# Half-size weight tiles, splits ordered by a clock in the source, and an x scaled by its norm's factor, in a two-layer decoder trunk on one core

## The chip, the cores and the metric

The kernel runs on one core of one Trainium2 chip. A core has a matrix engine (TensorE, PE in the profile, with its weight loads as PEld), a vector engine (DVE), an activation engine (ACT), GpSimd (POOL) and a queue that issues transfers (SP, shown as SPq). Each engine works through its own list of instructions in the order in which the source emits them, and waits on semaphores where one needs the result of another. The metric is the time of one execution on the device in microseconds (us); lower is better.

## The reference

Two layers are applied to 256 tokens of 1024 columns, all in float32. What matters here:

```python
for i in range(DEPTH):
    g = norm_gains[i]
    f = swiglu(rmsnorm(h, g[0]), ffn_gate[i, 0], ffn_up[i, 0], ffn_down[i, 0])
    h = h + MACARON * rmsnorm(f, g[1])
    mix = hybrid_mixer(rmsnorm(h, g[2]), ...)
    h = h + rmsnorm(mix, g[3])
    f = swiglu(rmsnorm(h, g[4]), ffn_gate[i, 1], ffn_up[i, 1], ffn_down[i, 1])
    h = h + MACARON * rmsnorm(f, g[5])
    gate = jax.nn.sigmoid(rmsnorm(h, g[6]) @ w_ple_gate[i])
    h = h + rmsnorm((p[i].astype(h.dtype) @ w_ple[i]) * gate, g[7])

def swiglu(x, w_gate, w_up, w_down):
    return (jax.nn.silu(x @ w_gate) * (x @ w_up)) @ w_down
```

A gated unit (`swiglu`) has weights of 1024 x 2816 (gate, up) and 2816 x 1024 (down); there are four of them. `rmsnorm` divides a row by its root mean square, so the factor is one number for each token.

## The kernel before

**Precision.** Every float32 product is made from three matmuls (`mm3`, L320). A weight tile `raw` (128 partitions x 1024 values) is split into a piece `hi` (ACT, L152) and a piece `lo` = raw - hi (DVE, L153); the activations are split likewise into `xh` and `xl` while they are transposed (`split_t`, L392: four transposes on PE, `hi` by ACT at L401, `lo` by DVE at L402). The product is xh*hi + xh*lo + xl*hi.

**Weights.** The class `Weights` (L97) streams them in the order of their use. There are four raw tiles of 1 MB; one load fills a tile with two pieces, and a tile is loaded anew when both have been split. A split piece lives in a slot: eight pairs of tiles, and two further pairs made from tiles that the mixer uses (L235), which are shut while the mixer runs. `need` splits a piece at once if a matmul is about to use it; `tick` splits the next one if a slot is free. Which step of which phase has a tick, and at which step other work is inserted, is written out by hand in the table `PLAN` (L52), and `run` (L325) follows it.

**A gated unit** (`ffn`, L433) goes over six chunks of the 2816 hidden columns: five of 512 and one of 256. T = 2 token tiles t of 128 rows. In each chunk of 512 there are six phases of 24 matmuls: gate t = 0 and 1 (pieces G0 to G3, two blocks of 128 inputs each), up t = 0 and 1 (U0 to U3), down t = 0 and 1 (D0 to D3). A phase runs in 8 steps of three matmuls; a slot comes free when the phase of t = 1 has used its piece. Gate ends in `silu` on ACT (L448), up in `hm` on DVE (L453); both multiply by `rx[t]`, the norm's factor of each token, because x itself is not scaled by it. `hid_t` transposes hm for the down phase.

The four units start in two ways. Unit 1 of layer 0 ("start") runs gate 0, gate 1, up 0, up 1 in its first chunk and has two insertions from the beginning of the program (`enter(1)` with the transposes of the second token tile). The other three ("first") run gate 0, up 0, gate 1, up 1, with the three insertions of `pending` (L388) that are left from the sublayer before. In them, gate 0 puts its xl matmuls last (`lo_last`, L418), with steps of two matmuls. After the first chunk of unit 1, `setup_late` (L289) loads masks and makes the rotary tables on DVE and ACT.

**Mixer and gate of the embeddings** (`mixer` L537, `ple` L774) use `run` and `PLAN` for their order, and the same slots.

```python
def tick(self):
    if self.can():
        self.prepare()
...
h1 = lambda: hid_t(1, hm1, nb)
if first:
    gate(0, c, pend[0], lo_last=True)
    hm0 = up(0, c, pend[1], pend[2])
    gate(1, c, h0)
    hm1 = up(1, c)
```

Of the kernel before, what the change touches and what calls it, by code (L numbers as in the profile page):

```python
# [36 lines left out]
NRAW = 4  # L37
CHUNKS = [(0, 512), (512, 512), (1024, 256), (1280, 512), (1792, 512), (2304, 512)]
# [58 lines left out]
class Weights:  # L97
# [3 lines left out]
    def __init__(self, nc, raw_pool, slots):  # L101
# [3 lines left out]
        self.shut = set()  # L105
        self.slot = {}
        self.specs = []
        self.loads = []
        self.raw = {}
        self.got = {}  # L110
        self.next = 0
        self.next_load = 0

    def add(self, keys, src, a, n):
        load = len(self.loads)
        self.loads.append((src, a * len(keys), n))
        for i, key in enumerate(keys):
            self.specs.append((key, load, i, a, n, i == len(keys) - 1))

    def load_one(self):  # L120
        i = self.next_load
        if i >= len(self.loads):
            return
        src, a, n = self.loads[i]
        raw = self.raw_pool.tile([P, 2048], F32, tag="raw", name=f"raw{i}")
        view = raw[:, : a * n].rearrange("p (a n) -> p a n", n=n)
        if i == 0:
            for j in range(0, a, a // 2):
                self.nc.sync.dma_start(view[:, j : j + a // 2], src[:, j : j + a // 2])
        else:  # L130
            self.nc.sync.dma_start(view, src)
        self.raw[i] = view
        self.next_load += 1

    def pick(self):
        return next((i for i in self.free if i not in self.shut), None)

    def can(self):
        return self.next < len(self.specs) and self.pick() is not None

    def prepare(self):
        key, load, part, a, n, last = self.specs[self.next]
        while self.next_load <= load:
            self.load_one()
        raw = self.raw[load][:, part * a : (part + 1) * a, :]
        slot = self.pick()
        self.free.remove(slot)
# [3 lines left out]
        hv, lv = (v.rearrange("p (a n) -> p a n", n=n) for v in (hi, lo))  # L151
        self.nc.scalar.activation(hv, raw, AF.Copy)  # L152
        self.nc.vector.tensor_tensor(lv, raw, hv.bitcast(F32), op=ALU.subtract)  # L153
        self.got[key] = (hv, lv)
        self.next += 1
        if last:
            del self.raw[load]
            self.load_one()
# [4 lines left out]

    def need(self, key):
        while key not in self.got:
            assert self.can(), (key, self.specs[self.next])
# [9 lines left out]
def hybrid_block(ctx: ExitStack, tc: tile.TileContext, a, out):  # L176
# [53 lines left out]
    ones = const.tile([1, P], F32, name="ones")  # L230
    nc.gpsimd.memset(ones, 1.0)

# [1 line left out]
    slots = [((piece_pool, f"hi{i}", 1024), (piece_pool, f"lo{i}", 1024)) for i in range(NS)]  # L234
    slots += [((work, "kdt", 1024), (work, "grp", 1024)), ((work, "vm", T * H * VW), (work, "vd", T * H * VW))]  # L235
    W = Weights(nc, raw_pool, slots)
    for l in range(DEPTH):
        for f in range(2):
            if f == 1:
# [3 lines left out]
                def add_in(name, c0, n):  # L243
                    for j in range(2):
                        W.add([(l, name, 2 * j), (l, name, 2 * j + 1)], win[:, 4 * j : 4 * j + 4, c0 : c0 + n], 2, n)

                add_in("A", 0, ZA)
                add_in("dq", ZA, 512)
                W.add([(l, "qu", 0), (l, "qu", 1)], a["w_q_up"][l].rearrange("(k p) n -> p k n", p=P), 1, 768)
                W.add([(l, "kvu", 0)], a["w_kv_up"][l].rearrange("(k p) n -> p k n", p=P), 1, 1024)  # L250
                add_in("dk", ZA + 512, 512)
                add_in("dv", ZA + 1024, 512)
                for half in range(2):
                    for n in range(2):
                        W.add([(l, "wo", half, n, 0), (l, "wo", half, n, 1)],
                              wo[:, 4 * half : 4 * half + 4, n * 512 : (n + 1) * 512], 2, 512)
            wg = a["ffn_gate"][l, f].rearrange("(k p) n -> p k n", p=P)
            wu = a["ffn_up"][l, f].rearrange("(k p) n -> p k n", p=P)
            wd = a["ffn_down"][l, f].rearrange("(k p) n -> p k n", p=P)
            for c, (f0, w) in enumerate(CHUNKS):  # L260
                ka = 1024 // w
                for name, src in (("G", wg), ("U", wu)):
                    for j in range(KD // (2 * ka)):
                        W.add([(l, f, c, name, 2 * j), (l, f, c, name, 2 * j + 1)],
                              src[:, 2 * ka * j : 2 * ka * (j + 1), f0 : f0 + w], ka, w)
                for j in range(w // 256):
                    k0 = f0 // P + 2 * j
                    W.add([(l, f, c, "D", 2 * j), (l, f, c, "D", 2 * j + 1)], wd[:, k0 : k0 + 2, :], 1, 1024)
        gt = a["w_ple_gate"][l].rearrange("(k p) n -> p k n", p=P)
        for n in range(2):  # L270
            for j in range(2):
                W.add([(l, "gt", n, 2 * j), (l, "gt", n, 2 * j + 1)],
                      gt[:, 4 * j : 4 * j + 4, n * 512 : (n + 1) * 512], 2, 512)
            if n == 0:
                W.add([(l, "pe", 0), (l, "pe", 1)], a["w_ple"][l].rearrange("(k p) n -> p k n", p=P), 1, 1024)

    for i in range(NRAW):
        if i == 2:
# [10 lines left out]
    def setup_late():  # L289
        """Masks and rotary tables."""  # L290
# [51 lines left out]
    def rstd(ss, ns, tag="rs", eps=EPS):  # L342
        """(ss / n + eps) ** -0.5 for each column of ss."""
# [25 lines left out]
    def post(t, f, gain, q, gain_pre):  # L369
        """h[t] += norm(f) / q; gives h[t] * gain_pre, and what does the second half of the columns."""  # L370
# [36 lines left out]
    def proj(ps, t, keys, fin, cols=None, k0=0, first=True, last=True, sh=None, sl=None, lo_last=False):  # L407
        """ps += x[t] @ w over the pieces named by keys."""
# [4 lines left out]
        for i, key in enumerate(keys):  # L413
            wh, wl = W.need(key)
            na = wh.shape[1]
            for j in range(na):
# [493 lines left out]
```

## Time and profile before

| | |
|---|---|
| median of the runs | 1053.22 us (2 runs, 1052.02 and 1054.42) |
| span of the profiled execution | 1052.4 us |
| PE busy | 1037.1 us, 5168 matmuls |
| PEld busy | 867.0 us |
| DVE busy | 645.8 us, 819 instructions |
| ACT busy | 528.9 us, 744 instructions |
| POOL busy | 51.1 us |
| transfers | 189.02 MB, mean 180 GB/s |

The times are of one profiled execution, in microseconds from its first instruction. The page gives no time of this execution other than its span; the span lies between the two timed runs, 0.8 us below their median. A row of a group gives line, engine, operation, output and inputs by the program's names, how many, the busy time and the mean of one in ns, and the idle time of that engine just before, with what ended it. A row of a timeline gives the start, the length, and the instruction; rows of the same instruction in succession are merged ("x4"), and idle time before it stands in brackets.

### The profile page before, as it was taken

Reading aid. Unit: us, or ns where it says so; the run is one execution under the profiler, and the core shown is the slowest. Engines: PE = TensorE matmul, PEld = TensorE weight load, DVE = VectorE, ACT = ScalarE, POOL = GpSimd, SP = SyncE. Lnnn points to the kernel's source line nnn. Section 1 sums busy time; section 2 is a strip of 40 time slices with the busy share of each in tenths; the row PEclk is TensorE's granted clock in tenths of the full one; section 3 lists DMA queues with packets and bytes.
Section 4 is the critical chain, followed back from the end, with each engine's and each line's share of the span. In section 5 each row is a group of like instructions: output and inputs, shape, how many; then the busy total and the mean of one; then the engine's idle time right before and its main releaser. Section 6 shows DMA issues by size and latency. Waiting matters only on the chain.

```text
span 1052.4 us, 13069 instructions
## 1 busy us (share of the span) xinstructions
PE 1037.1 (99%) x5168; PEld 867.0 (82%) x5168; DVE 645.8 (61%) x819; ACT 528.9 (50%) x744; POOL 51.1 (5%) x123
## 2 busy tenths in 40 slices
PE   8999999999999999999999999999999999999997
PEld 5889888878888898888878888888888888988886
DVE  4765554778677455456776545557877864555474
ACT  5544443555556444444665444445564654444463
POOL 0000000210020000000110000002000200000011
PEclk9999999999999999999999999999999999999999
DMA  8864546364227564554547645455532575545601
GB/s 321 304 227 168 193 164 211 106 222 160 82 94 272 191 213 160 201 200 160 200 160 259 212 169 200 153 163 168 180 120 82 190 275 184 198 162 172 227 21 40
DMA packets 86158, 189.02 MB, mean 180 GB/s; under 512 B 3665, under 2 KB 15313, under 8 KB 86098
## 3 DMA queue, kind: packets, MB, share of 16 engines
q1 hardware_dynamic: 86098, 188.20, 52.0%
q8 instruction: 40, 0.66, 0.2%
q14 instruction: 20, 0.16, 0.0%
HBM read 187.13 MB, written 1.05 MB: 179 GB/s over the span
## 4 chain that ended last, share of the span: by engine, by line
PE 92%; DVE 3%; ACT 2%; DMA 1%; issue 1%; POOL 0%; SPq 0%; DVEq 0%; POOLq 0%; ACTq 0%
PE acc L479 23%; PE u L323 8%; PE u L321 8%; PE u L322 8%; PE g L321 7%; PE g L323 7%; PE g L322 7%; PE tp L398 3%; PE o L706 2%; PE sc L666 1%; DVE lo L153 1%; PE gt L323 1%; PE gt L322 1%; PE gt L321 1%; PE f L321 1%; PE f L323 1%
## 5 line engine op out<-in xcount | busy, mean ns | idle before, releaser
L153 DVE TENSOR_TENSOR lo<-raw,hi 128x1024 fp32r<-128x1024 f32 (+1 forms) x338 | 405.1, 1214 | 204.2 <-ACT hi L152 194.1
L152 ACT ACTIVATE hi<-raw 128x1024 fp32r<-128x1024 f32 (+1 forms) x338 | 347.2, 1049 | 170.9 <-PE u L323 79.3
L479 PE MATMUL acc<-hi,hid 128*128 128x512 f32 x704 | 201.5, 392 | 0.0
L479 PEld LDWEIGHTS acc<-hi,hid 128*128 128x128 f32 x704 | 131.7, 188 | 27.4
L321 PE MATMUL u<-hi,xh 128*128 128x512 f32 (+1 forms) x384 | 145.3, 379 | 0.0
L323 PE MATMUL u<-hi,xl 128*128 128x512 f32 (+1 forms) x384 | 143.2, 373 | 0.0
L322 PE MATMUL u<-lo,xh 128*128 128x512 f32 (+1 forms) x384 | 143.0, 372 | 0.0
L321 PE MATMUL g<-hi,xh 128*128 128x512 f32 (+1 forms) x360 | 135.0, 375 | 2.3 <-ACT xh L401 2.3
L323 PE MATMUL g<-hi,xl 128*128 128x512 f32 (+1 forms) x360 | 134.6, 374 | 0.0
L322 PE MATMUL g<-lo,xh 128*128 128x512 f32 (+1 forms) x360 | 134.5, 374 | 0.0
L479 PE MATMUL acc<-lo,hid 128*128 128x512 f32 x352 | 118.3, 395 | 0.0
L323 PEld LDWEIGHTS u<-hi,xl 128*128 128x128 f32 x384 | 72.3, 188 | 13.0
L322 PEld LDWEIGHTS u<-lo,xh 128*128 128x128 f32 x384 | 72.4, 188 | 12.1
L321 PEld LDWEIGHTS u<-hi,xh 128*128 128x128 f32 x384 | 72.3, 188 | 12.0
L321 PEld LDWEIGHTS g<-hi,xh 128*128 128x128 f32 x360 | 68.5, 190 | 14.4 <-ACT xh L401 2.7
L322 PEld LDWEIGHTS g<-lo,xh 128*128 128x128 f32 x360 | 68.5, 190 | 12.3 <-DVE lo L153 0.5
L323 PEld LDWEIGHTS g<-hi,xl 128*128 128x128 f32 x360 | 68.4, 190 | 12.4 <-DVE xl L402 0.6
L479 PEld LDWEIGHTS acc<-lo,hid 128*128 128x128 f32 x352 | 66.2, 188 | 13.2
L401 ACT ACTIVATE hid<-tp 128x512 fp32r<-128x512 f32 (+1 forms) x48 | 27.0, 563 | 95.6 <-PE tp L398 95.6
L453 DVE SCALAR_TENSOR_TENSOR hm<-u,rs,silu 128x512 f32<-128x512 f32 (+1 forms) x48 | 33.7, 703 | 65.1 <-PE u L323 65.1
L448 ACT ACTIVATE silu<-g,rs 128x512 f32<-128x512 f32 (+1 forms) x48 | 31.3, 652 | 81.3 <-PE g L323 81.2
L402 DVE TENSOR_TENSOR hid<-tp,hid 128x512 fp32r<-128x512 f32 (+1 forms) x48 | 31.0, 647 | 44.0 <-ACT hid L401 43.6
(216 smaller groups left out, 1195.0 us busy)
## 6 DMA issues: line engine op xcount, KB each, us to landing
raw<-in_ffn_up SPq DMA_DIRECT2D x44, 1024.0 KB, 5.1
raw<-in_ffn_down SPq DMA_DIRECT2D x44, 1024.0 KB, 5.0
raw<-in_ffn_gate SPq DMA_DIRECT2D x43, 1024.0 KB, 5.2
raw<-in_w_in SPq DMA_DIRECT2D x12, 1024.0 KB, 5.2
raw<-in_w_out SPq DMA_DIRECT2D x8, 1024.0 KB, 5.1
raw<-in_w_ple_gate SPq DMA_DIRECT2D x8, 1024.0 KB, 5.1
gain<-in_norm_gains SPq DMA_DIRECT2D x15, 512.0 KB, 4.0
raw<-in_w_in SPq DMA_DIRECT2D x4, 832.0 KB, 5.2
```

Source lines behind the costliest of these rows:

```text
L152: self.nc.scalar.activation(hv, raw, AF.Copy)
L153: self.nc.vector.tensor_tensor(lv, raw, hv.bitcast(F32), op=ALU.subtract)
L321: nc.tensor.matmul(ps, sh, wh, start=first, stop=False)
L322: nc.tensor.matmul(ps, sh, wl, start=False, stop=False)
L323: nc.tensor.matmul(ps, sl, wh, start=False, stop=last)
L398: nc.tensor.transpose(ps[:, j * P : (j + 1) * P], src[:, (b0 + j) * P : (b0 + j + 1) * P], ident)
L401: nc.scalar.activation(hv, v, AF.Copy)
L402: nc.vector.tensor_tensor(dl[:, k0 + b0 : k0 + b0 + nb, :], v, hv.bitcast(F32), op=ALU.subtract)
L448: nc.scalar.activation(s[:, :w], ps[:, :w], AF.Silu, scale=rx[t][:, 0:1])
L453: nc.vector.scalar_tensor_tensor(hm[:, :w], ps[:, :w], rx[t][:, 0:1], sg[t][:, c0 : c0 + w], op0=ALU.mult, op1=ALU.mult)
L479: nc.tensor.matmul(accs[t][n], hid[t][x][:, b, :], ws[w][:, 0, n * 512 : (n + 1) * 512], start=first and x + w == 0, stop=final and x == 1)
L706: nc.tensor.matmul(dst, pt[:, b * P : (b + 1) * P], va[:, kb, hd, :], start=kb == 0, stop=kb == t)
```

## The change

Six things are changed. No unit of the list `UNITS` has the kind "s", so the branches for it, and the functions `product`, `strassen` and `down_pairs` that belong to it, emit nothing.

1. Raw tiles are 0.5 MB and there are eight (`NRAW`), each for one piece, with one load each.
2. The two further slots are gone: eight slots everywhere, and a freed slot goes to the end of the list where the lowest number was taken before.
3. In the gated units `run` and `PLAN` give way to `flow` and `pump`. After each step `pump` moves a clock `pe` on by the step's nominal length, and splits pieces while a second clock `dve`, which counts nominal DVE work, is not over half a microsecond ahead of `pe`, a slot is free and the piece is not needed more than 11 us later (its `at` less 5). `need` still splits at once what is about to be used. Mixer and `ple` keep `run` and `PLAN`.
4. In each unit's first chunk `scaled` spreads `rx[t]` over the partitions with two float32 matmuls of a matrix of ones and a diagonal, and makes xs[t] = (xh + xl) * rx.
5. `sums` makes four sums and differences of halves of xs and splits each. What it writes is read only by `product`.
6. `rescale(t)` splits xs[t] anew into xh[t] and xl[t], and from the second chunk on `silu` and `hm` do without the factor.

```diff
-NRAW = 4
+NRAW = 8
+MM = 0.227
+UNITS = [("c", 0, 512), ("c", 512, 512), ("c", 1024, 256), ("c", 1280, 512), ("c", 1792, 512), ("c", 2304, 512)]
...
 class Weights:
...
     def load_one(self):
         i = self.next_load
-        if i >= len(self.loads):
+        if i >= len(self.loads) or not self.raw_free:
             return
         src, a, n = self.loads[i]
-        raw = self.raw_pool.tile([P, 2048], F32, tag="raw", name=f"raw{i}")
+        slot = self.raw_free.pop(0)
+        raw = self.raw_pool.tile([P, 1024], F32, tag=f"raw{slot}", name=f"raw{i}", bufs=1)
...
     def prepare(self):
...
         self.nc.scalar.activation(hv, raw, AF.Copy)
         self.nc.vector.tensor_tensor(lv, raw, hv.bitcast(F32), op=ALU.subtract)
+        self.dve += 1.2
...
+    def pump(self, us):
+
+        self.pe += us
+        self.dve = max(self.dve, self.pe - 1.0)
+        while self.can() and self.dve <= self.pe + 0.5:
+            spec = self.specs[self.next]
+            if spec[7] is not None and (self.pe < spec[7] - 5.0 or self.pe < self.ready.get(spec[4], -99.0)):
+                return
+            self.prepare()
...
     def finish(self, key):
         self.free.append(self.slot.pop(key))
-        self.free.sort()
...
-slots += [((work, "kdt", 1024), (work, "grp", 1024)), ((work, "vm", T * H * VW), (work, "vd", T * H * VW))]
...
+    def flow(gen, *inserts):
+
+        inserts = list(inserts)
+        n = 0
+        for us in gen:
+            n += 1
+            while inserts and inserts[0][0] <= n:
+                inserts.pop(0)[1]()
+            W.pump(us)
+        for _, fn in inserts:
+            fn()
...
-            nc.scalar.activation(s[:, :w], ps[:, :w], AF.Silu, scale=rx[t][:, 0:1])
+            nc.scalar.activation(s[:, :w], ps[:, :w], AF.Silu, scale=rx[t][:, 0:1] if c == 0 else 1.0)
...
+        def scaled():
+
+            rb = bank("rb")
+            dg = k2("dg")
+            for t in range(T):
+                nc.scalar.activation(dg[:, t * P : (t + 1) * P], ident, AF.Copy, scale=rx[t][:, 0:1])
+            for t in range(T):
+                nc.tensor.matmul(rb[:, t * P : (t + 1) * P], ones, dg[:, t * P : (t + 1) * P], start=True, stop=True)
+            for t in range(T):
+                xs[t] = k4("xs").rearrange("p (k q) -> p k q", q=P)
+                nc.vector.tensor_tensor(xs[t], xh[t].bitcast(F32), xl[t].bitcast(F32), op=ALU.add)
+                nc.vector.tensor_tensor(xs[t], xs[t], rb[:, None, t * P : (t + 1) * P].to_broadcast([P, KD, P]), op=ALU.mult)
+            W.dve += 4.9
+
+        def split_x(dh, dl, src):
+            nc.scalar.activation(dh, src, AF.Copy)
+            nc.vector.tensor_tensor(dl, src, dh.bitcast(F32), op=ALU.subtract)
+            W.dve += 0.7 * src.shape[1] / 4
+
+        def sums():
...
+            for name, i0, i1, op in (("P5", x21, x22, ALU.subtract), ("P6", None, x11, ALU.subtract), ("P7", x11, x21, ALU.subtract),
+                                     ("P3", x12, None, ALU.add)):
+                i0 = views["P5"] if name == "P6" else i0
+                i1 = views["P6"] if name == "P3" else i1
+                nc.vector.tensor_tensor(views[name], i0, i1, op=op)
+                W.dve += 0.7
+                split_x(*S[name], views[name])
+
+        def rescale(t):
+            split_x(xh[t], xl[t], xs[t])
...
-            if first:
-                gate(0, c, pend[0], lo_last=True)
-                hm0 = up(0, c, pend[1], pend[2])
-                gate(1, c, h0)
-                hm1 = up(1, c)
+            if c == 0 and len(pend) == 3:
+                gate(0, c, (1, pend[0]), lo_last=True)
+                hm0 = up(0, c, (2, pend[1]), (6, pend[2]))
+                gate(1, c, (4, h0), (6, scaled))
+                hm1 = up(1, c, (1, sums), (7, lambda: rescale(0)))
+            elif c == 0:
+                gate(0, c, (7, pend[0]), (7, pend[1]))
+                gate(1, c)
+                hm0 = up(0, c, (1, scaled), (4, sums))
+                hm1 = up(1, c, (6, h0), (7, lambda: rescale(0)))
...
+            flow(down(0, c, nb, 0, False), (5 * nb // 4, h1), (5 * nb // 4, lambda: rescale(1) if c == 0 else None))
+            flow(down(1, c, nb, 0, False))
```

More of the change, by code (lines that the diff above doesn't have):

```diff
@@ L97 @@
 class Weights:
+    LAND = 8.5
     def __init__(self, nc, raw_pool, slots):
@@ L112, in __init__, with add, plan @@
         self.next_load = 0
[L114 to L118, printed above, removed]
+        self.pe = self.dve = 0.0
+        self.ready = {}
+    def add(self, key, src, a, n, load=None, plus=None, then=None, at=None):
+        self.specs.append((key, src, a, n, load or key, plus, then, at))
+    def plan(self):
+        for key, src, a, n, load, plus, then, at in self.specs:
+            for name, blocks in ((load, src), plus or (None, None)):
+                if name is None:
+                    continue
+                if name not in self.load_of:
+                    self.load_of[name] = len(self.loads)
+                    self.loads.append((blocks, a, n))
+                    self.uses.append(0)
+                self.uses[self.load_of[name]] += 1
@@ L132, in load_one, with used @@
-        self.raw[i] = view
-        self.next_load += 1
-    def pick(self):
-        return next((i for i in self.free if i not in self.shut), None)
+        self.nc.sync.dma_start(view, src)
+        self.raw[i], self.raw_slot[i] = view, slot
+        self.next_load += 1
+    def used(self, load):
+        self.uses[load] -= 1
+        if self.uses[load] == 0:
+            del self.raw[load]
+            self.raw_free.append(self.raw_slot.pop(load))
+            self.load_one()
     def can(self):
-        return self.next < len(self.specs) and self.pick() is not None
+        return self.next < len(self.specs) and bool(self.free)
@@ L147, in prepare @@
-        self.free.remove(slot)
+        raw = self.raw[load]
+        slot = self.free.pop(0)
         self.slot[key] = slot
@@ L489, in ffn, with up @@
-        last = len(CHUNKS) - 1
-        for c, (f0, w) in enumerate(CHUNKS):
-            nb = w // P
-            first = c == 0 and len(pend) == 3
-            kind = "start" if c == 0 and not first else "first" if first else "last" if c == last else "mid" if w == 512 else "small"
+        def up(t, c, *inserts):
+            w = UNITS[c][2]
+            ps = bank("u")
+            keys = [(l, f, c, "U", j) for j in range(w // 128)]
+            flow(proj(ps[:, :w], t, keys, t == 1), *inserts)
+            hm = k2("hm")
+            if c == 0:
+                nc.vector.scalar_tensor_tensor(hm[:, :w], ps[:, :w], rx[t][:, 0:1], sg[t][:, :w], op0=ALU.mult, op1=ALU.mult)
+            else:
+                nc.vector.tensor_tensor(hm[:, :w], ps[:, :w], sg[t][:, :w], op=ALU.mult)
+            W.dve += 0.7 * w / 512
+            return hm
@@ new lines, in hid_t, with down_mm, down @@
+        def hid_t(t, hm, nblk, into=None):
+            into = into or hid
+            split_t(hm, nblk, into[t][0], into[t][1])
+            W.dve += 0.65 * nblk / 4
+        def down_mm(t, n, x, w, b, hs, ws, first, final):
+            nc.tensor.matmul(accs[t][n], hs[t][x][:, b, :], ws[w][:, 0, n * 512 : (n + 1) * 512],
+                             start=first and x + w == 0, stop=final and x == 1)
+        def down(t, c, nb, b0, end, hs=None):
+            hs = hs or hid
+            halves = [[0], [1]] if end else [[0, 1]]
+            for ns in halves:
+                for b in range(nb):
+                    ws = W.need((l, f, c, "D", b0 + b))
+                    i = 0
+                    for x, w in ((0, 0), (0, 1), (1, 0)):
+                        for n in ns:
+                            down_mm(t, n, x, w, b, hs, ws, c == 0 and b == 0, end and b == nb - 1)
+                            i += 1
+                            if i % 3 == 0:
+                                if t == 1 and i == 3 * len(ns) and ns[-1] == 1:
+                                    W.finish((l, f, c, "D", b0 + b))
+                                yield 3 * MM
@@ L848, in hybrid_block @@
     for n in range(2):
-        nc.tensor.matmul(gain0[n], ones, row[:, n * 512 : (n + 1) * 512], start=True, stop=True)
+        nc.tensor.matmul(gain0[n], ones[:1], row[:, n * 512 : (n + 1) * 512], start=True, stop=True)
     def enter(t):
```

280 lines of the change are left out of this document (188 added, 92 removed).

## The prediction

> **What bounds the kernel now.** I read the page's busy line and its chain of work first, then the stretches of one first chunk, then the groups, and last the timelines of DVE, ACT and PE where the change inserts work.
>
> ```profile
> PE 1037.1 (99%) x5168; PEld 867.0 (82%) x5168; DVE 645.8 (61%) x819; ACT 528.9 (50%) x744; POOL 51.1 (5%) x123
> ...
> PE 92%; DVE 3%; ACT 2%; DMA 1%; issue 1%; POOL 0%; SPq 0%; DVEq 0%; POOLq 0%; ACTq 0%
> ```
>
> PE is busy for 1037.1 of 1052.4 us, and the chain that ended last is PE for 92%. All idle time of PE together is 15.3 us, so that is the most that any better order can give back. The stretches of unit 2's first chunk (PE, PEld, DVE, ACT, POOL busy, clock, share and GB/s of the transfers) are gate 1, up 1, and the two down phases:
>
> ```profile
> 323.60:329.50 5.90, 5.90 (x29) 4.88 (x28) 3.88 (x5) 2.92 (x5) 0.74 (x2) 1.00 0.94 330
> 329.50:335.00 5.50, 5.50 (x26) 4.53 (x26) 3.80 (x5) 4.71 (x5) 0.00 (x0) 1.00 0.40 122
> 335.00:346.40 11.40, 11.40 (x54) 9.38 (x52) 8.51 (x9) 6.74 (x7) 0.00 (x0) 1.00 0.95 346
> ```
>
> PE never pauses there, at a granted clock of 1.00. DVE has 16.19 us of work in 22.80 us: it has 6.6 us to spare in this stretch, though over the whole span it has 400. What the change adds to DVE must be held against the 6.6.
>
> **The durations.** Groups, with count, then busy time and mean ns of one, then idle time before them:
>
> ```profile
> L153 DVE TENSOR_TENSOR lo<-raw,hi 128x1024 fp32r<-128x1024 f32 (+1 forms) x338 | 405.1, 1214 | 204.2 <-ACT hi L152 194.1
> L402 DVE TENSOR_TENSOR hid<-tp,hid 128x512 fp32r<-128x512 f32 (+1 forms) x48 | 31.0, 647 | 44.0 <-ACT hid L401 43.6
> L381 DVE TENSOR_TENSOR xn<-h,gain 128x512 f32<-128x512 f32 x28 | 19.4, 694 | 1.0
> L692 DVE TENSOR_TENSOR pt<-pt,mult 128x512 f32<-128x512 f32 x8 | 4.9, 679 | 0.0
> L152 ACT ACTIVATE hi<-raw 128x1024 fp32r<-128x1024 f32 (+1 forms) x338 | 347.2, 1049 | 170.9 <-PE u L323 79.3 <-PE acc L479 59.2 <-PE g L323 22.9
> L312 ACT ACTIVATE tab<-turns 128x96 f32<-128x96 f32 x1 | 0.3, 284 | 0.5 <-DVE turns L311 0.5
> L849 PE MATMUL gain<-row,ones 1*128 1x512 f32 x4 | 3.7, 1089 | 2.2 <-DMA row<-in_norm_gains 2.2
> ```
>
> Now the timeline of the same stretch, first DVE, then ACT, then PE:
>
> ```profile
> 325.01 1.23 DVE L153 TENSOR_TENSOR lo<-raw,hi 128x1024 fp32r<-128x1024 f32 x1 [0.40 <-ACT hi L152]
> 327.60 0.69 DVE L402 TENSOR_TENSOR hid<-tp,hid 128x512 fp32r<-128x512 f32 x1 [1.36 <-ACT hid L401]
> 328.54 1.23 DVE L153 TENSOR_TENSOR lo<-raw,hi 128x1024 fp32r<-128x1024 f32 x1 [0.25 <-ACT hi L152]
> 331.46 4.68 DVE L153 TENSOR_TENSOR lo<-raw,hi 128x1024 fp32r<-128x1024 f32 x4 [1.70 <-ACT hi L152]
> 336.06 0.74 DVE L453 SCALAR_TENSOR_TENSOR hm<-u,rs,silu 128x512 f32<-128x512 f32 x1
> ...
> 326.96 0.60 ACT L401 ACTIVATE hid<-tp 128x512 fp32r<-128x512 f32 x1 [1.99 <-PE tp L398]
> 327.46 1.05 ACT L152 ACTIVATE hi<-raw 128x1024 fp32r<-128x1024 f32 x1
> ...
> 326.33 0.60 PE L398 MATMUL tp<-ident,hm 128*128 128x128 f32 x4
> 326.68 0.48 PE L321 MATMUL g<-hi,xh 128*128 128x512 f32 x1
> 328.16 0.40 PE L321 MATMUL g<-hi,xh 128*128 128x512 f32 x1
> 328.85 0.39 PE L321 MATMUL g<-hi,xh 128*128 128x512 f32 x1
> 329.54 0.39 PE L321 MATMUL u<-hi,xh 128*128 128x512 f32 x1
> 330.22 0.39 PE L321 MATMUL u<-hi,xh 128*128 128x512 f32 x1
> ```
>
> A step of three matmuls is 0.68 us (329.54 to 330.22), a phase 5.45. A DVE operation on 1024 columns takes 1.16 in a row (four in 4.68), on 512 columns 0.69 with its latency and about 0.60 in a row. The row of L692 reads PSUM and a broadcast tile, and takes no longer than L381, which reads neither: the multiplication by the broadcast factor in `scaled` gets no surcharge.
>
> **Added to the first chunk: three units that begin with `pending`.** `scaled` is four DVE operations on 1024 columns, 4 x 1.16 = 4.7. `sums` is four rounds, and each is a chain: the sum on DVE (0.69), its hi on ACT (0.60), its lo on DVE (0.65). DVE works in order, so it waits for ACT within each round, as the row of L402 shows (43.6 us of idle time before 48 of them, after ACT's hid): 1.95 a round with the gaps of a few hundredths, 7.8 in all, where the source's clock counts 5.6. `rescale` is 1.05 on ACT and 1.16 on DVE for each t. Together DVE's queue grows by 4.7 + 7.8 + 2.3 = 14.8 us, against 6.6 of slack. Pieces split ahead would cover the rest, but with eight slots G0 to G3 and U0 to U3 fill them all when gate 1 begins. D0 and D1 follow when G0 and G1 come free, at steps 3 and 5. G2 is free only after step 6, where `scaled` is inserted, so D2 and D3 stand behind `scaled`, `sums`, `rescale(0)` and hm1 in DVE's queue, wherever `pump` or `need` puts them.
>
> I walk through unit 2 on the axis above. (a) At the end of step 6 (328.16) PE comes to the two matmuls of `scaled`, which wait for two small ACT operations (0.3 each, by L312) behind D1's hi (to 328.5): 329.2. The matmuls have 128 columns each; a quarter of L849's 1.09 would be 0.27, a transpose of the same width 0.11 (four in 0.36 before the next matmul starts); I take 0.23 each. PE continues at 329.65, 1.5 late. (b) DVE ends D1's lo at 329.7, `scaled` at 334.4, `sums` at 342.2; ACT gives rescale(0)'s hi at 342.55, DVE its lo at 343.75, hm1 at 344.4, D2's lo at 345.6. PE has 14 steps (two of gate 1, eight of up 1, four of down 0) and is at D2 at 339.2, does two matmuls with D2's hi, and needs its lo from 339.65 on (that the hi itself comes only at 343.6 changes nothing): it waits 5.95. (c) Then come the last matmul of step 5, the transposes of hm1 (to 346.3) and step 6 (to 347.0). ACT has hid1 to 346.9, rescale(1) to 347.9, D3's hi to 348.95; DVE D3's lo at 350.3. PE needs it at 347.45: 2.85. Chunk 1's G0 to G3 are split by 350.3 + 4 x 1.16 = 354.9, and PE gets there after 0.9 and 5.45, at 356.65: no wait, with 1.7 to spare. Sum 1.5 + 5.95 + 2.85 = 10.3, three times 30.9.
>
> **The first unit of all.** Its order is another, and its setup follows the first chunk.
>
> ```profile
> 16.00 1.28 DVE L854 TENSOR_TENSOR xn<-h,gain 128x512 f32<-128x512 f32 x2
> ...
> 25.40 0.39 PE L321 MATMUL u<-hi,xh 128*128 128x512 f32 x1
> ...
> 48.60 0.57 SPq L292 DMA_DIRECT2D mask<-in_mask  x1
> ...
> 55.14 0.29 DVE L297 CAST mask<-mask 128x256 bf16<-128x256 f32 x1 [5.70 <-DMA mask<-in_mask]
> ...
> 58.91 0.28 ACT L312 ACTIVATE tab<-turns 128x96 f32<-128x96 f32 x1 [0.50 <-DVE turns L311]
> ```
>
> U0 and U1 are now split ahead of `enter(1)`, which ends 2.3 later; its transposes wait 1.1. Up 0 then begins at 26.5 (25.40 before). After step 1 the matmuls of `scaled` stand behind silu 1 (0.67) and two small ones: 0.6 and 0.45. DVE does `scaled` to 31.75, `sums` to 39.55, hm0 to 40.2; PE wants hm0 at 37.1: 3.1. Then hid0, rescale(0) and hm1 come before D0, whose lo ends at 45.3 where PE wants it at 42.4: 2.9. D3 waits for hid1 and rescale(1) as above: 2.85. That is 11.0. Of chunk 1 only G0 to G2 are issued before `setup_late`; G3 stands behind it on ACT and DVE. Their lo ends at 56.1; the mask's transfer, queued on SP behind loads that wait for these splits, starts at 56.5; in the rows above the mask is read 6.5 after its issue and the tables end 4.05 later: 67.1, then G3's lo at 69.3. PE needs it at 63.3: 6.0. Before, ten slots covered that wait, which is seen as DVE's 5.70. Sum 17.0.
>
> **Two slots fewer elsewhere.** By the source's order, followed piece by piece, five pieces were ready at the entry of unit 3 (after `ple`); with eight slots it is three, G0 to G2, and `pump` issues G3 only after the first insertion.
>
> ```profile
> 533.08 2.00 ACT L152 ACTIVATE hi<-raw 128x1024 fp32r<-128x1024 f32 x2
> ...
> 533.23 0.39 PE L419 MATMUL g<-hi,xh 128*128 128x512 f32 x1
> ...
> 536.15 1.22 DVE L153 TENSOR_TENSOR lo<-raw,hi 128x1024 fp32r<-128x1024 f32 x1
> ```
>
> 533.23 is step 7, which takes G3. Its hi comes at 534.1, its lo, in the place of the one at 536.15, at 537.3, and the matmul that wants it would have started at 533.46: 3.9. At the entries of units 2 and 4 (after the mixer) G0 to G3 and U0 are ready. In the mixer the slots were eight before.
>
> **What costs nothing.** Loads of 0.5 MB: twice as many on SP, which has room, and eight pieces of 2.72 us each (four steps) lie between a load and its use.
>
> ```profile
> ACT hi L152 <- DMA raw<-in_ffn_gate: 7.4, 2, 6.4
> ...
> raw<-in_ffn_up SPq DMA_DIRECT2D x44, 1024.0 KB, 5.1
> ```
>
> A load lands in 5.1 us, and ACT waited for one only twice, 7.4 us in all. If that cover went, each late load would hold ACT and then PE. `silu` and `hm` without the factor keep their length (L453's kind took 0.74, a plain one 0.69). The clock in the later chunks issues every piece at least 3.4 us of PE before its use, against 2.3 for hi and lo: nothing.
>
> **Sum.** 30.9 + 17.0 + 3.9 = 51.8. Against the execution shown (span 1052.4) that gives 1104.2; the median of the runs is 0.8 above that span: 1105.
>
> **The rivals.** *Hidden after all* (0.08): DVE goes only from 61% to 66% (645.8 and 4 x 12.4 of busy time), so the added work vanishes and only the eight small matmuls and ACT's delay ahead of them remain, 4 x 1.5: 1059. For it: DVE's 204.2 us of idle time before lo. Against it: the order of DVE's queue and the 6.6. It decides if D2's lo ends by 339.65, that is, if 6 us fewer stand ahead of it. *More waits in chunk 1* (0.12): there the margin is 1.7; if `scaled` or `sums` takes over 1.7 longer than I count, that comes once more for G0 to G3; a multiplication of twice the length (2.3 for two) gives 4 x 2.3: 1114, and up to 1120 with both. *Faster* (0.02): an order that takes away all of PE's idle time gives 1053.2 - 15.3 = 1038, if no insertion delays PE. PE's own rows speak against it: the idle time lies at the beginning, at the end and around the mixer. [...] *Loads too slow* (0.02): a chunk of 512 needs 12 pieces, 6.3 MB, in 32.7 us, 192 GB/s; the rows above show 346 GB/s. Halving the load must cost nearly half of the rate before PE waits; at 150 GB/s each chunk takes 9 us longer, 22 chunks give 198: 1250. [...]
>
> **How the numbers follow.** The forecast has 0.76. Low end: the setup's wait at 3 instead of 6, and the rounds of `sums` overlapped to the 5.0 of their DVE time, 4 x 2.8: 1105 - 3 - 11.2 = 1091; with errors of a few us in each walk, 1080. High end 1120. Outside lie the hidden case, faster, slow loads, and a few in a hundred more. A measurement of this kernel can tell some 2% (21 us) from no change. Slower by over 2% (1074): 0.76 + 0.12 + 0.02 less 0.02 for a walk that is off by 30: 0.88; within 2%: 0.10; faster: 0.02.
>
> **What would show it.** Right: gaps on PE in each unit's first chunk alone, after the second block of down 0 and before the fourth, released by DVE lo; about 10 us a unit; in the first unit one more in gate 0 of chunk 1, behind the mask; in unit 3 one in gate 0. DVE's busy time up by some 50 us, in blocks after gate 1. Wrong: `sums` in much under 7.8 us, PE without a gap in down 0 of the first chunk, waits for transfers of raw, or gaps in chunks 2 to 5.

## The result, and the profile after

The changed kernel takes 1135.51 us in the median (two runs, 1134.83 and 1136.20) against 1053.22: a ratio of 1.078, with a 95% interval of 1.075 to 1.082. Slower was forecast, and slower it is, but 30 us beyond the forecast and 15 beyond the top of the range.

| | before | after |
|---|---|---|
| median of the runs | 1053.22 us | 1135.51 us |
| span of the profiled execution | 1052.4 us | 1133.1 us |
| mean granted TensorE clock in it | 0.999 | 0.976 |
| PE busy | 1037.1 us | 1066.7 us |
| PE idle (span less busy) | 15.3 us | 66.4 us |
| DVE busy | 645.8 us | 684.5 us |

The page of the changed kernel (busy line; the clock granted in 40 slices, in tenths; groups with their idle time and its releaser):

```profile
PE 1066.7 (94%) x5184; PEld 879.2 (78%) x5184; DVE 684.5 (60%) x875; ACT 529.6 (47%) x776; POOL 62.5 (6%) x123
...
PEclk9999999999999799999998999999999989999999
...
L562 PE MATMUL acc<-hi,hid 128*128 128x512 f32 x704 | 213.0, 409 | 22.0 <-ACT hi L177 21.2
...
L562 PE MATMUL acc<-lo,hid 128*128 128x512 f32 x352 | 124.0, 412 | 5.4 <-DVE lo L178 5.4
```

The extra 80.6 us of span are two things. PE is idle for 51.1 us more. It is also busy for 29.6 us more, although it has only 16 matmuls more, of 128 columns each. That second number is the first sign of something that the forecast had left out: the clock line dips in three slices, and the mean clock fell to 0.976.

To see where the time arises, I compared the start of every phase on PE in the two traces; each entry is the growth of the delay over that stage:

| stage | grew by, us | forecast |
|---|---|---|
| unit 1, first chunk and the chunk after it | 19.7 | 17.0 |
| units 2 to 4, the two matmuls of `scaled` | 1.3 + 1.3 + 1.3 | 4.5 |
| units 2 to 4, down phases of the first chunk | 12.9 + 11.5 + 11.4 | 26.4 |
| entry of unit 3 | 5.6 | 3.9 |
| the chunk of 256, four units | 1.2 each, 4.8 | 0 |
| the two mixers | 4.1 + 2.6 | 0 |
| `ple`, two layers | 2.4 + 2.4 | 0 |

The entries come to 81.3; many phases shorter by some hundredths make up the rest. Unit 2's first chunk holds the main mechanism. These are the same three stretches that the prediction shows of before (gate 1, up 1, the two down phases), now of the changed kernel:

```profile
348.47:355.73 7.26, 6.74 (x33) 5.33 (x32) 5.10 (x6) 3.62 (x7) 0.74 (x2) 1.00 0.56 189
355.73:361.20 5.47, 5.47 (x26) 4.51 (x25) 4.60 (x6) 1.32 (x2) 0.00 (x0) 1.00 0.32 94
361.20:385.52 24.32, 17.18 (x53) 12.14 (x52) 17.37 (x19) 12.17 (x14) 0.00 (x0) 0.72 0.38 130
```

The last stretch took 11.40 us and takes 24.32: PE is busy for 17.18 of it, at a mean clock of 0.72. The timeline of DVE over it, in the changed kernel, shows who holds what:

```profile
358.29 1.22 DVE L608 TENSOR_TENSOR xs<-xs,rb 128x1024 f32<-128x1024 f32 x1
359.54 0.69 DVE L627 TENSOR_TENSOR fP<-xs 128x512 f32<-128x512 f32 x1
360.93 0.69 DVE L613 TENSOR_TENSOR sP<-fP,sP 128x512 fp32r<-128x512 f32 x1 [0.70 <-ACT sP L612]
...
366.90 0.69 DVE L613 TENSOR_TENSOR sP<-fP,sP 128x512 fp32r<-128x512 f32 x1 [0.69 <-ACT sP L612]
367.85 1.23 DVE L613 TENSOR_TENSOR xl<-xs,xh 128x1024 fp32r<-128x1024 f32 x1 [0.25 <-ACT xh L612]
368.99 0.75 DVE L550 SCALAR_TENSOR_TENSOR hm<-u,rs,silu 128x512 f32<-128x512 f32 x1
369.65 1.22 DVE L178 TENSOR_TENSOR lo<-raw,hi 128x1024 fp32r<-128x1024 f32 x1
374.18 1.23 DVE L613 TENSOR_TENSOR xl<-xs,xh 128x1024 fp32r<-128x1024 f32 x1 [0.25 <-ACT xh L612]
```

`sums` runs from 359.54 to 367.59 (366.90 + 0.69): 8.05 us, of which each round waits 0.7 for ACT. Then come `rescale(0)`, hm1, and D2's lo at 369.65, in the order of the forecast. What PE made of it, in the same trace:

```profile
363.69 0.39 PE L562 MATMUL acc<-hi,hid 128*128 128x512 f32 x1
368.81 1.22 PE L562 MATMUL acc<-hi,hid 128*128 128x512 f32 x2 [4.73 <-ACT hi L177]
370.92 0.79 PE L562 MATMUL acc<-lo,hid 128*128 128x512 f32 x1 [0.89 <-DVE lo L178]
...
375.14 1.22 PE L562 MATMUL acc<-hi,hid 128*128 128x512 f32 x2 [1.30 <-ACT hi L177]
376.59 1.22 PE L562 MATMUL acc<-lo,hid 128*128 128x512 f32 x2 [0.23 <-DVE lo L178]
377.61 1.91 PE L562 MATMUL acc<-hi,hid 128*128 128x512 f32 x4
```

Both waits stand where the forecast put them, before D2 and before D3. But the last row is new: four matmuls in 1.91 us until the next group starts at 379.32 (1.71), where a matmul at full clock has a step of 0.227 (in this trace 0.68 for three, from 360.29 to 360.97). The same trace cut at the steps of the clock, into windows of 3.41 us (length, busy times of PE, PEld, DVE, ACT, POOL, then the granted clock):

```profile
364.78:368.19 3.41, 0.00 (x0) 0.00 (x0) 2.33 (x4) 2.05 (x4) 0.00 (x0) 1.00 0.00 0
368.19:371.61 3.42, 1.91 (x4) 1.01 (x5) 2.68 (x3) 0.57 (x1) 0.00 (x0) 0.50 0.01 2
371.61:375.02 3.41, 2.24 (x8) 1.42 (x6) 1.53 (x2) 2.42 (x4) 0.00 (x0) 0.50 0.52 154
375.02:378.43 3.41, 3.06 (x6) 2.00 (x7) 3.41 (x4) 3.41 (x5) 0.00 (x0) 0.50 0.20 28
378.43:381.85 3.42, 3.42 (x9) 2.64 (x8) 2.65 (x3) 0.98 (x2) 0.00 (x0) 0.50 1.00 372
381.85:385.26 3.41, 3.41 (x16) 2.82 (x15) 2.34 (x2) 1.58 (x2) 0.00 (x0) 1.00 0.96 359
```

In this trace the clock is 1.00 or 0.50, and its changes lie whole multiples of 3.413 us apart. PE was idle from 364.78 to 368.19 and got half the clock for the next four windows, until a window (378.43) in which it never paused. Nine matmuls were done there in the time of sixteen. From the first record of the clock in the trace (at 13.21) to the last matmul there are eight such drops (at 20.04, 47.34, 57.58, 238.49, 368.20, 579.82, 610.54 and 924.57), for 51.2 us together; in the kernel before, recorded from 16.43 on, there is none.

### The profile page after: what moved, and what is told of

Read it like the earlier page. It is cut to its first block, busy times and chain, and to the rows that moved or that the text cites. A ratio compares the mean times of both kernels' runs of the same rounds, so it can differ in the third digit from the quotient of the medians.

```text
span 1133.1 us, 13707 instructions
## 1 busy us (share of the span) xinstructions
PE 1066.7 (94%) x5184; PEld 879.2 (78%) x5184; DVE 684.5 (60%) x875; ACT 529.6 (47%) x776; POOL 62.5 (6%) x123
## 5 line engine op out<-in xcount | busy, mean ns | idle before, releaser
L178 DVE TENSOR_TENSOR lo<-raw,hi 128x1024 fp32r<-128x1024 f32 (+1 forms) x338 | 396.7, 1213 | 209.2 <-ACT hi L177 208.7
L177 ACT ACTIVATE hi<-raw 128x1024 fp32r<-128x1024 f32 (+1 forms) x338 | 335.6, 1044 | 25.0 <-PE za L399 7.5
L562 PE MATMUL acc<-hi,hid 128*128 128x512 f32 x704 | 213.0, 409 | 22.0 <-ACT hi L177 21.2
L562 PEld LDWEIGHTS acc<-hi,hid 128*128 128x128 f32 x704 | 136.7, 197 | 55.1 <-ACT hi L177 25.5
L562 PE MATMUL acc<-lo,hid 128*128 128x512 f32 x352 | 124.0, 412 | 5.4 <-DVE lo L178 5.4
L540 ACT ACTIVATE silu<-g 128x512 f32<-128x512 f32 (+1 forms) x40 | 22.2, 555 | 178.0 <-PE g L399 178.0
L452 POOL TENSOR_SCALAR ss<-ss 128x1 f32<-128x1 f32 x16 | 7.5, 466 | 751.7 <-ACT junk L442 748.3
```

Source lines behind the costliest of these rows:

```text
L452: nc.gpsimd.tensor_scalar(e[:, 0:1], e[:, 0:1], q * q / D, q * q * EPS, op0=ALU.mult, op1=ALU.add)
L540: nc.scalar.activation(s[:, :w], ps[:, :w], AF.Silu, scale=rx[t][:, 0:1] if c == 0 else 1.0)
L562: nc.tensor.matmul(accs[t][n], hs[t][x][:, b, :], ws[w][:, 0, n * 512 : (n + 1) * 512], start=first and x + w == 0, stop=final and x == 1)
```

## The experiments

The theory after the result: the order of DVE's queue decides. Where long work is put ahead of a split, PE waits; the clock makes each longer wait dearer; the same happens in small wherever the new clock in the source puts a split ahead of other work that PE wants. The rivals: the amount of work added is what counts; the loads or the slots cost; the clock costs nothing of its own.

**Without `sums`.**

```diff
-hm1 = up(1, c, (1, sums), (7, lambda: rescale(0)))
+hm1 = up(1, c, (7, lambda: rescale(0)))
...
-hm0 = up(0, c, (1, scaled), (4, sums))
+hm0 = up(0, c, (1, scaled))
```

> Leaves out the four sums of halves of xs and their splits, which nothing reads. Theory A (D2, D3 and hm1 wait on PE because sums and scaled stand ahead of them in DVE's queue, and PE's clock is halved after the longest of these waits): without the 7.8 us of sums D2 and D3 are split before PE wants them; units 2 to 4 keep only the 1.3 us of scaled's matmuls and unit 1 loses its waits for hm0, D0 and D3: about 1089 us, no half clock in units 2 to 4 but for the entry of unit 3. Theory B (the eight slots and the source's clock cause the loss, the added work is hidden): over 1120 us.

Measured: 1081.27 us (1079.62 to 1082.92), 1.026 of the kernel before (1.022 to 1.030). The theory's 1089 was 8 too high. `sums` alone is worth 54 us, the half clock that it brings included (mean granted clock 0.997, against 0.976 after the change). With 8 us fewer ahead of it, D2 comes in time, and the down phases of units 2 to 4 lose nothing; the setup's wait in unit 1 went with them.

**x not scaled at all**: `scaled`, `sums` and `rescale` out, the norm's factor in `silu` and `hm` of every chunk as before. The streaming of the weights, the eight slots and the clock in the source remain.

```diff
-gate(1, c, (4, h0), (6, scaled))
-hm1 = up(1, c, (1, sums), (7, lambda: rescale(0)))
+gate(1, c, (4, h0))
+hm1 = up(1, c)
```

> Leaves out scaled, sums and rescale; silu and hm take the norm's factor in every chunk, as in the kernel before. What is left is the half-size tiles, eight slots and the splits by the source's clock. Theory A: that part costs 28 us of the 82 (start and setup 8, small chunks 4.8, mixers 6, ple 4.7, entry of unit 3 5.6): about 1081 us. Theory B: over 1115 us. If the half-size tiles and the clock cost nothing, as the prediction had it for the later chunks: about 1062.

Measured: 1074.73 us (1074.49 to 1074.96), 1.020 (1.017 to 1.023). That is 6 below what was expected, since the setup does not wait here. So the scaling of x costs 60.8 us together, and the remaining parts of the change 21.5, where the forecast had 3.9 for the slots and 6.0 for the setup. The stages left in the trace: the entry of unit 3 (5.4), the chunk of 256 four times (1.25 each), the mixers (2.2 and 2.7), `ple` (2.4 each), and 1.0 at the start.

What the small ones are is seen in unit 1's chunk of 256, DVE in the changed kernel:

```profile
112.96 2.36 DVE L178 TENSOR_TENSOR lo<-raw,hi 128x1024 fp32r<-128x1024 f32 x2 [0.52 <-ACT hi L177]
115.24 0.42 DVE L552 TENSOR_TENSOR hm<-u,silu 128x256 f32<-128x256 f32 x1
```

and the same place in the kernel before:

```profile
93.74 0.48 DVE L453 SCALAR_TENSOR_TENSOR hm<-u,rs,silu 128x256 f32<-128x256 f32 x1 [0.95 <-PE u L323]
```

Before, DVE stood ready and waited for PE, so hm1 started 0.2 after the phase's end (93.53). Now two splits are in hand, and hm1 starts 2.05 after it (113.19). The splits come in good time for their own use; hm1, which PE wants next, comes late behind them. At the entry of mixer 1 it is the norm's own chain, DVE in the changed kernel:

```profile
222.74 2.35 DVE L178 TENSOR_TENSOR lo<-raw,hi 128x1024 fp32r<-128x1024 f32 x2
225.01 0.69 DVE L462 TENSOR_TENSOR y<-acc,gain 128x512 f32<-128x512 f32 x1
...
227.20 0.68 DVE L490 TENSOR_TENSOR xl<-tp,xh 128x512 fp32r<-128x512 f32 x1
```

and the same xl in the kernel before:

```profile
204.24 0.68 DVE L402 TENSOR_TENSOR xl<-tp,xh 128x512 fp32r<-128x512 f32 x1
```

In the changed kernel y, h, xn and the xl that PE waits for stand behind two splits. Before, the xl came 3.45 after the start of the mixer's first matmul on PE (204.24 against 200.79), now 5.7 (227.20 against 221.50): the 2.24 that the stage grew.

**The same work in another place.** First only `sums`, moved from up 1 of the first chunk to gate 1 of the second:

```diff
-hm1 = up(1, c, (1, sums), (7, lambda: rescale(0)))
+hm1 = up(1, c, (7, lambda: rescale(0)))
...
-gate(1, c)
+gate(1, c, *([(1, sums)] if c == 1 else []))
```

> All of the change's work, but sums is inserted in gate 1 of the second chunk and not in the first. Theory A (the place in DVE's queue counts, not the amount of work): as without sums, 1089 to 1094 us. If the amount of DVE work counts: as the changed kernel, over 1120.

Measured: 1087.05 us (1086.64 to 1087.46), 1.031 (1.028 to 1.034). In units 2 to 4 `sums` costs nothing there. In unit 1 it costs 7.6, because there it meets the setup's work on DVE; the mean granted clock of the run is 0.993, against 0.997 without `sums`. Then everything that the change adds, each part where DVE has room: `sums` in gate 1 of chunk 2 (in unit 1: of chunk 4), no splits in steps 5 to 8 of up 1 in the chunk of 256, none in steps 3 to 6 of the first phase of unit 1.

```diff
-    def pump(self, us):
+    def pump(self, us, quiet=False):
+        if quiet:
+            return
...
-gate(0, c, (7, pend[0]), (7, pend[1]))
+gate(0, c, (7, pend[0]), (7, pend[1]), quiet=(3, 4, 5, 6))
...
-gate(1, c)
+gate(1, c, *([(1, sums)] if c == (1 if len(pend) == 3 else 3) else []))
```

> All instructions of the change, with eight slots, in other places: sums in gate 1 of the second chunk (in unit 1 of the fourth), no split at steps 5 to 8 of up 1 in the chunk of 256, none at steps 3 to 6 of the very first phase. Theory (each loss is a place in DVE's queue): e4's 1087 less 7 (sums in unit 1 no longer meets the backlog of the setup), 5 (small chunks) and 1.5 (start): about 1073.5. Rival (the added DVE work itself has a price of its own): over 1083.

Measured: 1074.88 us (1074.79 to 1076.31), 1.019 (1.017 to 1.020). The instructions and slots are those of the change, and 60.6 us are gone. Its up 1, its two down phases and the gate phases after them in unit 2's first chunks:

```profile
335.19:340.63 5.44, 5.44 (x26) 4.50 (x24) 5.30 (x6) 4.48 (x5) 0.00 (x0) 1.00 0.32 95
340.63:352.05 11.42, 11.42 (x54) 9.44 (x53) 10.02 (x11) 7.23 (x8) 0.00 (x0) 1.00 0.64 194
352.05:362.93 10.88, 10.88 (x50) 9.01 (x49) 6.71 (x9) 3.44 (x5) 0.00 (x0) 1.00 0.84 280
```

The down phases take 11.42 us (11.40 before the change) without a pause and at full clock, with DVE at 15.3 of 16.9 us in up 1 and down. The timeline of DVE in the same trace:

```profile
341.14 0.74 DVE L552 SCALAR_TENSOR_TENSOR hm<-u,rs,silu 128x512 f32<-128x512 f32 x1
341.80 2.35 DVE L178 TENSOR_TENSOR lo<-raw,hi 128x1024 fp32r<-128x1024 f32 x2
...
358.79 0.69 DVE L615 TENSOR_TENSOR sP<-fP,sP 128x512 fp32r<-128x512 f32 x1 [2.77 <-ACT sP L614]
```

D2 and D3 are split by 344.15, and the later rounds of `sums` are still to come at 358.79, beside the gate phases of the next chunk, where PE does not pause either. The amount as a cause is ruled out. What is left, 20.6 us of span, is the entry of unit 3 (5.5), the mixers (2.7 each), `ple` (2.4 each), the matmuls of `scaled` (1.3 each in units 2 to 4) and 1.6 in unit 1; phases shorter by some hundredths take off the rest.

**The price of the half clock.** Dummy matmuls into a bank that nothing reads fill PE's waits ahead of the third and fourth block of down 0, in the first chunk of units 2 to 4. The waits themselves stay.

```diff
+if c == 0 and t == 0 and b >= 2 and len(pend) == 3:
+    dm, wd = bank("dm"), W.got[(l, f, c, "D", 1)][0]
+    for _ in range(22 if b == 2 else 8):
+        nc.tensor.matmul(dm, hs[t][0][:, 0, :], wd[:, 0, :512], start=True, stop=True)
```

> The changed kernel with 22 matmuls more ahead of the third block of down 0 in the first chunk of units 2 to 4, and 8 ahead of the fourth: they write a bank that nothing reads, and lie in the time in which PE waits for D2 and D3. If the halved clock comes from PE's idle time, the half clock in these three chunks goes and the time falls by 9 us although PE has 90 matmuls more: about 1126. If the halving has another cause: 1135 or more.

Measured: 1130.80 us (1130.34 to 1131.27), 1.073 (1.070 to 1.076). Unit 2's down phases with the dummies:

```profile
362.10:383.27 21.17, 19.04 (x83) 14.73 (x82) 16.90 (x19) 12.20 (x14) 0.00 (x0) 1.00 0.34 112
```

With 30 matmuls more they take 3.15 us less (24.32 after the change), at a clock of 1.00. The three units lose 9.77, 9.81 and 9.79 against 12.91, 11.54 and 11.39: the half clock cost 3.1, 1.7 and 1.6, 6.5 in all. The total came 5 above the expectation, though. The expectation had 9 for the half clock, not 6.5, and unit 1 lost 3.3 more, though its code is the same (mixer 1, also with the same code, lost 2.0 less than after the change, where one window of it, from 238.49, has half the clock). In unit 1 the windows of the clock lie 0.6 earlier (36.50 against 37.10). In both kernels PE waits for hm0, for the same time. PE in the changed kernel:

```profile
42.24 0.66 PE L486 MATMUL tp<-ident,hm 128*128 128x128 f32 x4 [3.58 <-DVE hm L550]
```

and with the dummies:

```profile
42.00 0.66 PE L486 MATMUL tp<-ident,hm 128*128 128x128 f32 x4 [3.58 <-DVE hm L550]
```

The two windows that hold this wait, after the change (columns as above):

```profile
37.10:40.51 3.41, 1.56 (x7) 0.94 (x6) 2.34 (x4) 0.97 (x2) 0.00 (x0) 1.00 0.00 0
40.52:43.93 3.41, 1.69 (x10) 1.44 (x10) 1.72 (x3) 1.27 (x3) 0.00 (x0) 1.00 0.00 0
```

and with the dummies, with the window that follows:

```profile
36.50:39.91 3.41, 1.91 (x9) 1.26 (x7) 2.59 (x4) 0.70 (x2) 0.00 (x0) 1.00 0.00 0
39.91:43.32 3.41, 1.32 (x8) 1.19 (x9) 1.35 (x2) 1.26 (x3) 0.00 (x0) 1.00 0.00 0
43.32:46.74 3.42, 2.46 (x6) 0.91 (x4) 3.17 (x4) 3.42 (x4) 0.00 (x0) 0.50 0.00 0
```

The grid cuts the wait at another point. After the change PE keeps 1.56 and 1.69 us of busy time in the two windows, and the clock stays; with the dummies 1.91 and 1.32, and it drops. From this wait on unit 1 loses the 3.3 us more.

**The tiles.** The kernel before, with eight raw tiles of 0.5 MB and one load for each, and nothing else of the change.

```diff
-NRAW = 4
+NRAW = 8
...
-raw = self.raw_pool.tile([P, 2048], F32, tag="raw", name=f"raw{i}")
+raw = self.raw_pool.tile([P, 1024], F32, tag="raw", name=f"raw{i}")
```

> The kernel before with eight raw tiles of 0.5 MB, one load for each piece, and nothing else. Theory (loads are covered): 1053 to 1054, same. Rival (smaller transfers cost bandwidth that PE feels): over 1070.

Measured: 1054.83 us (1052.56 to 1055.57, ten runs), 1.001 (1.000 to 1.002). Loads of half the size cost 2 us at most, by the interval.

**What remains without the scaling.** From here on x is unscaled, and one thing is added at a time. First no splits in a few steps: 5 to 8 of up 1 in the chunk of 256, and in the last chunk step 4 of down 0 and 6 to 8 of down 1, where the norm's chain is due.

```diff
-                 (nb + 1, h1))
+                 (nb + 1, h1), quiet=(4,))
...
-                 (nb + 2, lambda: x_t(0, xn0, 0)))
+                 (nb + 2, lambda: x_t(0, xn0, 0)), quiet=(6, 7, 8))
```

> e2 (x unscaled), and the clock issues no split at a few steps: steps 5 to 8 of up 1 in the chunk of 256, step 4 of the last down 0, steps 6 to 8 of the last down 1. Theory: in the changed kernel these splits stand on DVE ahead of hm1 and of the norm's work at the unit's end, and PE waits for those (1.25 in each of four units, 2.2 in each mixer, 0.8 and 1.6 in each ple): 1074.7 less 14.3, 1060. Rival: the splits only move, and PE waits for them later: 1070 to 1075.

Measured: 1071.88 us (1070.83 to 1072.94), 1.017 (1.015 to 1.020): 2.9 gained of the 14.3 expected, and in the rival's range. The aimed waits did go: the chunk of 256 loses nothing, the first wait of the mixers is gone, and `ple` went from 2.4 to 0.55. But, as the rival has it, the splits only moved: PE met a new wait for a lo in each mixer, and the stages grew by 4.5 and 5.5. PE in mixer 1 of this kernel:

```profile
210.82 0.40 PE L399 MATMUL dq<-hi,xh 128*128 128x512 f32 x1
215.92 0.80 PE L400 MATMUL dq<-lo,xh 128*128 128x512 f32 x1 [4.71 <-DVE lo L178]
```

and DVE there:

```profile
212.91 0.48 DVE L782 SCALAR_TENSOR_TENSOR ln<-za,rs,latg 128x256 f32<-128x256 f32 x1 [4.19 <-POOL rs L438]
...
214.65 1.22 DVE L178 TENSOR_TENSOR lo<-raw,hi 128x1024 fp32r<-128x1024 f32 x1
```

DVE stood idle for 4.19 us before an instruction that waited for POOL, with the lo that PE needed behind it (214.65): the lo waited too, and PE for 4.71. Next, two further slots, shut in the mixer, as the kernel before had them:

```diff
+slots += [((work, "kdt", 1024), (work, "grp", 1024)), ((work, "vm", T * H * VW), (work, "vd", T * H * VW))]
...
+        W.shut = {NS, NS + 1}
```

> e5, and the two further slots of the kernel before are back (shut in the mixer). Theory: G3 and U0 are ready when unit 3 begins, so its entry loses its 5.35 us: 1055. Rival: the wait at unit 3's entry comes from the clock that starts anew there, not from the slots: 1060.

Measured: 1065.24 us (1064.55 to 1067.53), 1.012 (1.009 to 1.014). The wait at the entry of unit 3 is gone and so is the new one in the mixers; at the ends of the units the norm's chain waits again (2.3 in each mixer, 2.2 in each `ple`). The total is 10 above the 1055, since the run with quiet steps, its base, was 12 above its own expectation. Then no splits in steps 3 to 6 of unit 1's first phase:

```diff
-gate(0, c, (7, pend[0]), (7, pend[1]))
+gate(0, c, (7, pend[0]), (7, pend[1]), quiet=(3, 4, 5, 6))
```

> e6, and in the very first phase no split is issued at steps 3 to 6, so that the second token tile's work does not stand behind those of U0 and U1. Theory: the 1.5 us of the start go, 1053 to 1054, level with the kernel before. Rival: the start is bound by the loads, and U0 and U1 come too late instead: 1055 to 1057.

Measured: 1063.32 us (1063.12 to 1063.74), 1.009 (1.007 to 1.011). The step gave 1.9 where 1.5 was expected; the total lies 10 above the expectation because its base did. Last, in the two last down phases the splits at the steps that the kernel before had in its table:

```diff
-                 (nb + 1, h1), quiet=(4,))
+                 (nb + 1, h1), ticks=(1, 3, 5, 7))
...
-                 (nb + 2, lambda: x_t(0, xn0, 0)), quiet=(6, 7, 8))
+                 (nb + 2, lambda: x_t(0, xn0, 0)), ticks=(5,))
```

> e7, and in the two down phases of a unit's last chunk the clock issues nothing: splits come at the steps that the kernel before has in its table (1, 3, 5, 7 of down 0 and 5 of down 1). Theory (in e7 the clock, with ten slots, still puts splits ahead of the norm's work at a unit's end: 2.9 in each mixer, 2.2 in each ple): 1063.3 less 10, about 1053, level with the kernel before or up to 2 below it, since the start is 1.7 earlier. Rival (the splits left out there are missed at the entry of the mixer): 1058 to 1063.

Measured: 1062.67 us (1060.09 to 1064.81), 1.009 (1.007 to 1.011), the same as the kernel ahead of it within the intervals, and in the rival's range. The waits moved instead of going: 1.6 in each `ple`, 3.0 and 3.7 at the two mixers, and the mean granted clock is 0.995, against 0.999 in the run ahead of it. These 10 us above the kernel before are not settled: which pieces would have to be ready at the unit's end, and in which order, was not found. The new order in which freed slots are taken again is in all of these runs, and was not tested by itself. No version ran faster than the kernel before.

## Why the prediction was wrong, and what it had right

The direction and the main mechanism were right. The time left the range by two terms that the forecast did not have: places in DVE's queue that it put at nothing, and the half clock.

**Right: the bound and the main mechanism.** PE bounds, and DVE's place in the queue, not its total, decides. The 14.8 us of new work against 6.6 of slack held: D2 and D3 stood behind `scaled`, `sums`, `rescale(0)` and hm1. At full clock the three down phases lose 9.8 each (the run with the dummies), against 8.8 forecast. `sums` took 8.05 (7.8 forecast), `scaled` 1.3 on PE (1.5). The rival *hidden after all* is half true: the added work on DVE can be hidden, with `sums` in chunk 2 (only the 1.3 of `scaled` on PE stays in units 2 to 4), but not where the change puts it. DVE's busy time grew by 38.7, where some 50 was to show. *More waits in chunk 1* did not come: the gate phase after the down phases loses 0.0 in units 2 to 4. *Loads too slow* fell with the run of half tiles (1054.83 us, 0.2% more at most by the interval). No run here shows the highest rate that loads of 0.5 MB reach; what the run shows is that this kernel's time hardly follows their size.

**Right in its waits: unit 1 and the entry of unit 3.** Unit 1's wait for hm0 was 3.58 (3.1 forecast), and those for D0 and D3 were 2.6 each (1.18 and 1.38, 1.87 and 0.72; forecast 2.9 and 2.85). The setup gave 3.0 instead of 6.0. The mask and the tables, DVE in the changed kernel:

```profile
65.71 0.29 DVE L373 CAST mask<-mask 128x256 bf16<-128x256 f32 x1 [5.46 <-DMA mask<-in_mask]
...
70.72 2.36 DVE L178 TENSOR_TENSOR lo<-raw,hi 128x1024 fp32r<-128x1024 f32 x2 [1.18 <-ACT hi L177]
```

and PE in the same trace:

```profile
68.69 0.39 PE L399 MATMUL g<-hi,xl 128*128 128x512 f32 x1
70.74 0.50 PE L397 MATMUL g<-hi,xh 128*128 128x512 f32 x1 [1.66 <-ACT hi L177]
72.00 0.50 PE L398 MATMUL g<-lo,xh 128*128 128x512 f32 x1 [0.76 <-DVE lo L178]
```

G3's split, the first of the last row of DVE, was later than forecast (71.9, forecast 69.3), but PE itself came to it only at 68.9 (68.69 and a step of 0.23) instead of 63.3. The entry of unit 3, PE in the changed kernel:

```profile
576.56 0.49 PE L507 MATMUL g<-hi,xh 128*128 128x512 f32 x1 [0.79 <-ACT hi L177]
579.80 0.80 PE L508 MATMUL g<-lo,xh 128*128 128x512 f32 x1 [2.75 <-DVE lo L178]
```

0.79 and 2.75 make 3.5. Each wait also costs the 0.16 by which a matmul of 0.39 is longer than the step of 0.23, and that gives the 3.9 of the forecast. The stage grew by 5.6, because the clock was at 0.50 from 579.82 to 583.23, which is half of 3.41 us of work: 1.7.

**Wrong: the step "What costs nothing".** Its sentence on the source's clock in the later chunks compared each piece with its own use: 3.4 us ahead against the 2.3 that it needs. That is true, and not enough. DVE took its queue in order (hm1 in unit 1's chunk of 256 started 2.05 after its phase, behind two splits), and what matters is also what the piece stands ahead of: hm1 in the chunk of 256 (4.8 us in four units), the norm's chain at the ends of the units (4.7 in `ple`, and in the mixers some 5.1 of their 6.7, the rest being half clock). Together 14.6 us where the forecast had none. The runs with quiet steps show it: with splits held back at those steps the chunk of 256 loses nothing, and the waits for the norm's chain go or shrink, though other waits come in their place.

**Wrong: the pace of PE after a wait.** Steps (a) to (c) let PE continue at 0.68 a step, read from a stretch in which PE never paused, and had no term for a slower clock. In the changed kernel PE's pauses brought another clock (0.50 after the wait for D2; 0.72 on average over unit 2's down phases, and 1.00 with the waits filled). In the down phases this cost 6.5 (shown by the dummies). In the five single windows elsewhere (three in unit 1, mixer 1, unit 3) half of the busy time of each is an estimate of some 8. Together about 14.5 us.

The sum closes: 51.8 forecast, 14.6 for the places left out, 14.5 for the clock, less 3.0 for the setup, and 3.0 because each down phase lost 1.0 more at full clock, make 80.9 against 80.6. That the last two cancel is chance. With only one of the two missing terms the time would have stayed just within the range (1105 and 14.6 make 1119.6, and its top is 1120); both together left it. The top had been drawn from *more waits in chunk 1*, a place that was looked at, and had nothing for the places that were not.

## What to carry to other kernels

When a piece of work is issued early on an engine that works through its queue in order, as DVE did here, ask two things: is it ready for its use, and what does it stand in front of. The second decided here, and what took `sums` off the path was another place in the queue, not less work. And when a change makes TensorE wait for most of one of the windows of 3.41 us seen here (a wait of 2.75 in a window with 0.52 of work was enough in unit 3), price the matmuls after the wait at half the pace, here 0.43 a step for 0.227, until a window of nearly full work has passed (in the changed kernel one with 3.16 us or more of PE's busy time).

## What the runs showed of the hardware

In the changed kernel the granted clock of TensorE was 1.00 or 0.50, and its changes lay on one grid of 3.413 us: from the drop at 20.04 to that at 924.57 are 904.53 us, 265 windows of 3.413. It dropped after the fully idle window at 364.78, but also after a window with the end of one wait and the whole of another, of 2.75, in it (576.41 to 579.82, PE busy for 0.52), while the 3.58 us wait of unit 1, divided between two windows, did not lower it, and did in the run with the dummies. A gap of 2.75 sufficed and one of 3.58 did not, so the length of the gap alone did not decide; PE's busy time within a window went better with the drops. In the changed kernel, every recorded window at full clock with less than 1.3 us of PE's modelled busy time was followed by half clock, and none with 1.69 or more; near 1.6 both occur (1.56 without a drop above; 1.61, from 235.08, with one). In the run with the dummies a window with 1.32 was followed by a drop and one with 1.91 was not. This measure gives no sharp bound.

Half clock also lasted: after the wait before D2 it held for four windows (13.65 us), with 1.91, 2.24, 3.06 and 3.42 us of PE's busy time: the end of the wait for D2's hi, that for its lo (0.89) and those for D3 (1.30 and 0.23) left pauses in the first three. The return needed no quite full window, though: in unit 1 it came after one with 3.16 (47.34 to 50.75). So one long wait and a short one soon after cost more than their sum: 12.9 in unit 2 for 9.8 us of waits.
